# Recurrence gates of a hybrid encoder block: two blocks side by side in the array's rows, their halves brought together by transfers within SBUF, and one square less

## The chip, the core and the metric

The kernel runs on one core of one Trainium2 chip. The metric is device time in microseconds. Three runs of the kernel before took 1136.99, 1137.01 and 1138.92 us, a median of 1137.01 us. One further execution was profiled: it took 1136.66 us, of which 1134.9 us are the span from the first to the last instruction of the program.

The engines are called TensorE (PE in the rows; PEld is its weight load), VectorE (DVE), ScalarE (ACT), GpSimd (POOL) and SyncE (SP). SyncE only issues transfers here; GpSimd clears a few columns and issues some transfers.

## The reference

One layer on 512 tokens of 1024 features, all in float32: a feed-forward half step, a mixer and a second feed-forward half step. The mixer projects the normed input to seven parts. Two of them are attended over a token grid; one goes through a depthwise convolution and then through two gated linear recurrences, one forward in time and one backward:

```python
def _rglru_scan(xc, w_gates, b_gates, lam):
    xb = xc.reshape(B_, S, LRU_BLOCKS, LRU_BLOCK)           # 16 blocks of 64 features
    gates = jnp.einsum('bsni,gnio->gbsno', xb, w_gates)     # each block has its own 64 x 64 weights
    gates = gates + b_gates[:, None, None, :]
    r = jax.nn.sigmoid(gates[0])
    i = jax.nn.sigmoid(gates[1])
    log_a = -LRU_C * r * jax.nn.softplus(-lam)
    a = jnp.exp(log_a)
    bx = jnp.sqrt(-jnp.expm1(2.0 * log_a)) * (i * xc)
    _, h = lax.associative_scan(_lin_combine, (a, bx), axis=1)   # h_t = a_t h_(t-1) + bx_t
```

The gates r and i are 64 x 64 products: features of one block only see features of the same block. The two directions have weights of their own, so that 2 directions x 2 gates x 16 blocks of 64 x 64 weights meet 512 tokens.

## The kernel before

Features lie on the 128 partitions, so that the 1024 features are 8 feature tiles (f = 0 to 7) of 128 x 512, each of two blocks. Matrices of float32 are split into a rounded part and a rest (wh and wl for weights, xh and xl or ch and cl for data), and every product is three matmuls: wh by xh, wh by xl, wl by xh (mm3, L144). Weights stream in pieces of 128 x 1024 through load_w (L132): a transfer by SyncE into wraw, ScalarE's copy to wh (L118), VectorE's difference to wl (L121). There are four buffers each of wh and wl, and three of wraw.

The stages are: first feed-forward, the projection to the recurrence's input (wxr, L645, one piece of 24 matmuls for each f), the projections of q, k and v in two halves (wqkv, L667 to L669, 24 matmuls for a piece), three gate projections, the output projection and the second feed-forward. The recurrence and the attention are generators ("lanes") that weave() advances by a few steps behind each piece of a projection, so many steps per piece as RATE tells (4 for "lru" behind a piece of wxr, 3 behind a piece of the first q, k and v). A scheduler sets the final order of each engine's instructions; every engine works its own list from top to bottom and waits at an instruction whose inputs or buffers are not there.

The recurrence is made in two parts of four feature tiles each (LRU_F = 4). In each, lru() (L584) first makes the gates of one f and direction after the other. For f and direction d it does for g = 0 (r) and g = 1 (i): three matmuls of the full array, whose weights are 128 x 128 with two 64 x 64 blocks on the diagonal and zeros beside them, into one of four aux banks of PSUM; one sigmoid by ScalarE out of that bank (L607). Then VectorE multiplies i by the convolved input (L612) and ScalarE makes th = tanh(8 sp r) (L614), with sp the softplus. After the eight pairs of gates come, for each, a = exp(-8 sp r) (L618), its square (L621), (a*a + 1) * th, which is 1 - a*a (L622); then the roots (L625), the product of root and gated input (L627) and the scans (L633, L635).

In the text a gate group is one f with one direction. The eight groups of the first part (tiles 0 to 3) stand between pieces of wxr for f = 5 to 7, those of the second part (tiles 4 to 7) between pieces 8 to 12 of q, k and v. ch and cl of a tile (L591) must be there before its groups, the bank must have been emptied by the sigmoid that used it last.

Of the kernel before, what the change touches and what calls it, by code (L numbers as in the profile page):

```python
# [9 lines left out]
F32 = mybir.dt.float32  # L10
F32R = mybir.dt.float32r
AF = mybir.ActivationFunctionType
# [4 lines left out]
P = 128  # L17
T = 512
# [34 lines left out]
GB_BATCH = (range(0, 4), range(4, 6), range(6, 7), range(7, 8))  # L53

LRU_F = 4

ATT_LAG = 1, 2

# [9 lines left out]
def block_kernel(ctx: ExitStack, tc, a, out):  # L68
# [18 lines left out]
    def big_t(dt=F32, shape=(P, T), n="b"):  # L87
        return big.tile(list(shape), dt, tag="big", bufs=NBIG, name=nm(n))
# [7 lines left out]
    def aux_t():  # L96
        return aux.tile([P, T], F32, tag="aux", name=nm("aux"))
# [34 lines left out]
    def load_w(src, n, act=True):  # L132
        raw = raw_t()
        H, L = hl_t()
        s = slice(0, n)
        ld = nc.sync.dma_start(raw[:, s], src[:, s])
        if nld[0] < 8:
            tc.keep_in_program_order(ld)
        nld[0] += 1
        with tc.high_priority():  # L140
            split(raw[:, s], H[:, s], L[:, s], act)
        return H, L
# [53 lines left out]
        nc.scalar.activation(r, ps, AF.Copy)  # L196
        return r, rcol, vx

    def after(i, prev):

        i, prev = getattr(i, "ins", i), getattr(prev, "ins", prev)
        tc.add_manual_dep(i, prev.name, mybir.DependencyInfo(
            mybir.DependencyClass.NoSync, mybir.DependencyReason.DATA), reason="order")


    mark = {}
# [341 lines left out]
    sp8 = const.tile([P, 16], F32, name="sp8")  # L548
    nc.vector.tensor_scalar(sp8, sp, 8.0, None, ALU.mult)
# [30 lines left out]


    last_act = [None]

    def lru(fs):  # L584
        un = []
        cuts = {}

        def cut(f):
            if f in fs:
                cuts[f] = big_t(F32R, n="ch"), big_t(F32R, n="cl")  # L590
                split(xc[f], *cuts[f])  # L591

        cut(fs[0])
        for f in fs:
            gH, gL = load_w(a["wgate"][f], T)
            cut(f + 1)
            cH, cL = cuts.pop(f)
            yield
            for d in range(2):
                rt = []  # L600
                for g in range(2):
                    q = d * 2 + g
                    s = slice(q * P, (q + 1) * P)
                    ps = aux_t()
                    mm3(ps, gH[:, s], gL[:, s], cH, cL, True, True)
                    t = big_t(n="gate")
                    i = nc.scalar.activation(t, ps, AF.Sigmoid, bias=small[:, C_BG + f * 4 + q : C_BG + f * 4 + q + 1])  # L607
# [4 lines left out]
                nc.vector.tensor_tensor(ix, ix, xc[f], ALU.mult)  # L612
                th = big_t(n="th")
                tanh = nc.scalar.activation(th, r, AF.Tanh, scale=sp8[:, f * 2 + d : f * 2 + d + 1])  # L614
# [287 lines left out]
def layouts(inp):  # L902
# [28 lines left out]
    bd = np.zeros((KT, P, 4, P), wg.dtype)  # L931
    for b in range(16):
        s = slice((b % 2) * 64, (b % 2) * 64 + 64)
        bd[b // 2, s, :, s] = wg[:, :, b].reshape(4, 64, 64).transpose(1, 0, 2)
    o["wgate"] = bd.reshape(KT, P, 4 * P)
    col = lambda v: np.asarray(v).reshape(-1, KT, P).transpose(2, 1, 0).reshape(P, -1)
    o["small"] = con(np.concatenate([
        col(f("norm_ffn1")[0]), col(f("norm_mix")[0]), col(f("norm_ffn2")[0]),
        col(f("conv_w")[0]), col(f("conv_b")[0]),
        col(f("lru_b_gates")[0].reshape(4, D)), col(f("lru_lambda")[0]),  # L940
        np.tile(f("q_norm")[0], 2)[:, None], np.tile(f("k_norm")[0], 2)[:, None]], 1))


# [31 lines left out]
```

## Time and profile before

| what | value |
|---|---|
| median of three runs | 1137.01 us |
| the profiled execution, span of it | 1136.66 us, 1134.9 us |
| TensorE busy in the span | 1126.8 us (99%) |
| VectorE, ScalarE, GpSimd busy | 837.1, 617.3, 19.3 us |
| matmuls on the program's lines | 6874 |
| first part of the gates (from the first gate matmul to the first of q, k and v) | 384.21 to 409.58 us |
| second part (first to last gate matmul) | 453.1 to 480.3 us |

The profile's page sums up each engine's busy time, follows the chain of work that ended last back from the end, and lists the costliest groups of instructions with the mean of one. Other views show the same execution by stretches of time, by tile, or in order of time with the start of each instruction. A matmul's duration there includes the time in which it passes through the array, while the next has started; what one costs in a stream is the distance between two starts. A released wait stands in brackets behind the row.

### The profile page before, as it was taken

The numbers are of one execution on the slowest core, as the hardware profiler recorded it, in microseconds if no ns is written. First come the engines' busy times: TensorE is split into PE (matmuls) and PEld (weight loads), VectorE is DVE, ScalarE is ACT, GpSimd is POOL, SyncE is SP. The second block draws the span as 40 slices with busy tenths as digits, with TensorE's granted clock in tenths as the row PEclk, the third lists the DMA queues.
The fourth block names the chain that finished last, engine by engine and source line by source line (L and its number), as shares of the span: only waits on it lengthen the run. The fifth ranks groups of instructions, "written<-read, shape, count | busy, mean of one in ns | idle before, by whom it ended". The sixth has DMA issues, their size and how long they took to land.

```text
span 1134.9 us, 17275 instructions
## 1 busy us (share of the span) xinstructions
PE 1126.8 (99%) x6874; PEld 994.4 (88%) x6874; DVE 837.1 (74%) x1288; ACT 617.3 (54%) x924; POOL 19.3 (2%) x52
## 2 busy tenths in 40 slices
PE   9999999999999999999999999999999999999998
PEld 7899999988888888888788887778999999998886
DVE  7898888884836779788855577758688888894542
ACT  8554544563624696995564266756445545464330
POOL 0000000000000000010110000000000000000000
PEclk9999999999999999999999999999999999999999
DMA  8242333443333352353443232345123333253421
GB/s 274 81 131 80 122 97 109 132 133 103 121 102 104 98 169 68 124 165 93 137 143 103 93 102 90 107 167 186 56 80 124 95 108 116 89 171 94 130 75 38
DMA packets 43554, 130.70 MB, mean 115 GB/s; under 512 B 5968, under 2 KB 8272, under 8 KB 43472
## 3 DMA queue, kind: packets, MB, share of 16 engines
q1 hardware_dynamic: 39600, 119.36, 33.6%
q0 software_dynamic: 3296, 9.97, 2.9%
q8 instruction: 54, 0.88, 0.3%
q10 hardware_dynamic: 576, 0.26, 0.1%
q14 instruction: 28, 0.23, 0.1%
HBM read 121.17 MB, written 8.39 MB: 114 GB/s over the span
## 4 chain that ended last, share of the span: by engine, by line
PE 95%; DVE 3%; ACT 2%; issue 0%; DMA 0%; DVEq 0%; ACTq 0%
PE acc L260 29%; PE acc L146 11%; PE acc L145 11%; PE acc L147 10%; PE aux L260 5%; PE aux L145 4%; PE aux L146 4%; PE aux L147 4%; PE acc L668 3%; PE acc L667 3%; PE acc L669 3%; PE aux L796 1%; DVE wl L121 1%; PE aux L785 1%; DVE so L769 1%; ACT wh L118 1%
## 5 line engine op out<-in xcount | busy, mean ns | idle before, releaser
L118 ACT ACTIVATE wh<-wraw 128x1024 fp32r<-128x1024 f32 (+3 forms) x242 | 241.4, 1000 | 323.5 <-PE acc L260 98.5
L121 DVE TENSOR_TENSOR wl<-wraw,wh 128x1024 fp32r<-128x1024 f32 (+3 forms) x254 | 291.5, 1151 | 131.0 <-ACT wh L118 130.4
L260 PE MATMUL acc<-s,wh 128*128 128x256 f32 x1216 | 220.6, 283 | 0.0
L260 PEld LDWEIGHTS acc<-s,wh 128*128 128x128 f32 x1216 | 188.8, 190 | 0.0
L260 PE MATMUL acc<-s,wl 128*128 128x256 f32 x608 | 172.1, 283 | 0.0
L145 PE MATMUL acc<-xh,wh 128*128 128x512 f32 x304 | 120.4, 396 | 0.0
L146 PE MATMUL acc<-xl,wh 128*128 128x512 f32 x304 | 119.5, 393 | 0.0
L147 PE MATMUL acc<-xh,wl 128*128 128x512 f32 x304 | 118.9, 391 | 0.0
L260 PEld LDWEIGHTS acc<-s,wl 128*128 128x128 f32 x608 | 115.8, 190 | 0.0
L260 PE MATMUL acc<-xh,wl 128*128 128x256 f32 x304 | 86.1, 283 | 0.0
L260 PE MATMUL acc<-xl,wh 128*128 128x256 f32 x304 | 86.1, 283 | 0.0
L260 PE MATMUL acc<-xh,wh 128*128 128x256 f32 x304 | 86.0, 283 | 0.0
L667 PE MATMUL acc<-wh,xh 128*128 128x512 f32 x192 | 75.5, 393 | 0.0
L668 PE MATMUL acc<-wh,xl 128*128 128x512 f32 x192 | 74.8, 390 | 0.0
L669 PE MATMUL acc<-wl,xh 128*128 128x512 f32 x192 | 74.8, 389 | 0.0
L294 DVE TENSOR_TENSOR wraw<-wraw,pair 128x1024 f32<-128x1024 f32 x57 | 69.6, 1221 | 0.8
L145 PE MATMUL aux<-hh,wh 128*128 128x512 f32 x176 | 68.5, 389 | 0.0
L146 PE MATMUL aux<-hl,wh 128*128 128x512 f32 x176 | 68.5, 389 | 0.0
L147 PE MATMUL aux<-hh,wl 128*128 128x512 f32 x176 | 68.5, 389 | 0.0
L146 PE MATMUL acc<-hl,wh 128*128 128x512 f32 x176 | 68.5, 389 | 0.0
L145 PE MATMUL acc<-hh,wh 128*128 128x512 f32 x176 | 68.5, 389 | 0.0
L147 PE MATMUL acc<-hh,wl 128*128 128x512 f32 x176 | 68.5, 389 | 0.0
(195 smaller groups left out, 2221.5 us busy)
## 6 DMA issues: line engine op xcount, KB each, us to landing
wraw<-wqkv SPq DMA_DIRECT2D x24, 512.0 KB, 3.6
wraw<-wg SPq DMA_DIRECT2D x24, 512.0 KB, 3.5
wraw<-w1d SPq DMA_DIRECT2D x22, 512.0 KB, 3.6
wraw<-w2d SPq DMA_DIRECT2D x22, 512.0 KB, 3.6
pair<-w2s SPq DMA_DIRECT2D x20, 512.0 KB, 3.6
wraw<-w2s SPq DMA_DIRECT2D x20, 512.0 KB, 3.6
wraw<-w1s SPq DMA_DIRECT2D x18, 512.0 KB, 3.6
pair<-w1s SPq DMA_DIRECT2D x18, 512.0 KB, 3.6
```

The source lines that it names most:

```text
L118: nc.scalar.activation(H, raw, AF.Copy)
L121: nc.vector.tensor_tensor(L, raw, H.bitcast(F32), ALU.subtract)
L145: nc.tensor.matmul(ps, wh, xh, start=first, stop=False)
L146: nc.tensor.matmul(ps, wh, xl, start=False, stop=False)
L147: nc.tensor.matmul(ps, wl, xh, start=False, stop=last)
L260: nc.tensor.matmul(o, w_[:, c], x_, start=first and m + k == 0 and w_ is H and x_ is xh_, stop=m + k == 4 and w_ is L, skip_group_check=True)
L294: nc.vector.tensor_tensor(t, t, o, ALU.add)
L667: nc.tensor.matmul(pss[j], xh[kk][:, tj], H[:, s], start=kk == 0, stop=False)
L668: nc.tensor.matmul(pss[j], xl[kk][:, tj], H[:, s], start=False, stop=False)
L669: nc.tensor.matmul(pss[j], xh[kk][:, tj], L[:, s], start=False, stop=kk == KT - 1)
L769: nc.vector.tensor_tensor_reduce(so[:, cs], ps[hp][:, cs], bm[:, BTYPE[n]], -1.0, 3.0e38, ALU.add, ALU.min, nmx[:, i : i + 1])
L785: nc.tensor.transpose(pT[:, q * P : (q + 1) * P], pt[:, q * P : (q + 1) * P], ident)
```

## The change

Four things change in lru() and in the layout of two inputs.

1. The gate weights hold no zeros any more: wgate[f] is 128 x 256 in place of 128 x 512, with block 2f in rows 0 to 63 and block 2f + 1 in rows 64 to 127, and the 64 columns of r beside the 64 of i for each direction. A gate group is now three pairs of matmuls. The two of a pair have 64 rows each, use rows 0 to 63 and rows 64 to 127 of the array, and write two PSUM banks, one for each block: the bank of block b holds r of that block in its upper 64 partitions and i in its lower 64. The two of a pair and the three pairs are held in that order; the first also waits until the banks of the group before the last are both empty.
2. The two sigmoids of a group go to the two halves of one tile `both` (128 x 2 x 512, from the four buffers of the tag "pair"), which holds r above i for one block and for the other. Four transfers of 64 x 512 each, issued by GpSimd, bring them to r and i of the whole feature tile.
3. The product of i and the input and the tanh of a group are written out two groups later (LRU_LAG = 2).
4. tanh has half the argument, th = tanh(4 sp r) = (1 - a) / (1 + a), so that 1 - a*a = th * (1 + a)^2. VectorE multiplies the gated input by (a + 1) where it multiplied th before, the root is taken of th itself, and the square of a is gone. The biases are laid out to match.

```diff
@@ lru
-            gH, gL = load_w(a["wgate"][f], T)
+            gH, gL = load_w(a["wgate"][f], 2 * P)
...
             for d in range(2):
-                rt = []
-                for g in range(2):
-                    q = d * 2 + g
-                    s = slice(q * P, (q + 1) * P)
-                    ps = aux_t()
-                    mm3(ps, gH[:, s], gL[:, s], cH, cL, True, True)
-                    t = big_t(n="gate")
-                    i = nc.scalar.activation(t, ps, AF.Sigmoid, bias=small[:, C_BG + f * 4 + q : C_BG + f * 4 + q + 1])
+                c = slice(d * P, (d + 1) * P)
+                ps = [aux_t() for _ in range(2)]
+                mm = None
+                for W, X in ((gH, cH), (gH, cL), (gL, cH)):
+                    for b in (0, 1):
+                        o = slice(b * HD, (b + 1) * HD)
+                        prev, mm = mm, nc.tensor.matmul(
+                            ps[b], W[o, c], X[o], start=W is gH and X is cH, stop=W is gL)
+                        if prev is not None:
+                            after(mm, prev)
+                        elif len(evicted) > 1:
+                            after(mm, evicted[-2], True)
+                q = C_BG + f * 4 + d * 2
+                both = pair_t()
+                for b in range(2):
+                    i = nc.scalar.activation(both[:, b], ps[b], AF.Sigmoid, bias=small[:, q + b : q + b + 1])
                     if last_act[0] is not None:
                         after(i, last_act[0])
-                    rt.append(t)
-                r, ix = rt
-                nc.vector.tensor_tensor(ix, ix, xc[f], ALU.mult)
-                th = big_t(n="th")
-                tanh = nc.scalar.activation(th, r, AF.Tanh, scale=sp8[:, f * 2 + d : f * 2 + d + 1])
-                un.append((f, d, r, ix, th))
+                evicted.append(i)
+                r, ix = (big_t(n="gate") for _ in range(2))
+                for g, t in enumerate((r, ix)):
+                    for b in range(2):
+                        nc.gpsimd.dma_start(t[b * HD : (b + 1) * HD], both[g * HD : (g + 1) * HD, b])
+                got.append((f, d, r, ix))
+                if len(got) > LRU_LAG:
+                    tanh = use(*got.pop(0))
                 yield
+        for t in got:
+            tanh = use(*t)
+        yield
         for f, d, r, ix, th in un:
             exp = nc.scalar.activation(r, r, AF.Exp, scale=sn8[:, f * 2 + d : f * 2 + d + 1])
             after(exp, tanh)
-            sq = big_t(n="a2")
-            nc.scalar.activation(sq, r, AF.Square)
-            nc.vector.scalar_tensor_tensor(th, sq, 1.0, th, ALU.add, ALU.mult)
+            nc.vector.scalar_tensor_tensor(ix, r, 1.0, ix, ALU.add, ALU.mult)
```

In use() stand the product of ix with xc[f] and the tanh with sp4 = 4 sp in place of sp8.

Three places of the new order bear on the prediction. The numbers in the names tell the tiles of one program apart.

TensorE, the first gate groups, tile 0 with both directions (ch_624 and cl_625 are its two parts, aux the banks). Before:

```order
L145 MATMUL aux_631_3914<-ch_624_3900,wh_627_3905 128x512
L145 MATMUL aux_633_3920<-ch_624_3900,wh_627_3905 128x512
L145 MATMUL aux_636_3929<-ch_624_3900,wh_627_3905 128x512
L145 MATMUL aux_638_3935<-ch_624_3900,wh_627_3905 128x512
L146 MATMUL aux_631_3914<-cl_625_3901,wh_627_3905 128x512
L147 MATMUL aux_631_3914<-ch_624_3900,wl_628_3906 128x512
L146 MATMUL aux_633_3920<-cl_625_3901,wh_627_3905 128x512
```

Now:

```order
L618 MATMUL aux_631_3914<-ch_624_3900,wh_627_3905 128x512
L618 MATMUL aux_632_3915<-ch_624_3900,wh_627_3905 128x512
L618 MATMUL aux_636_3931<-ch_624_3900,wh_627_3905 128x512
L618 MATMUL aux_637_3932<-ch_624_3900,wh_627_3905 128x512
L618 MATMUL aux_631_3914<-cl_625_3901,wh_627_3905 128x512
L618 MATMUL aux_632_3915<-cl_625_3901,wh_627_3905 128x512
L618 MATMUL aux_631_3914<-ch_624_3900,wl_628_3906 128x512
L618 MATMUL aux_632_3915<-ch_624_3900,wl_628_3906 128x512
```

The number of gate matmuls is the same, 96. Those that follow each other now form pairs. They stand in 11 runs between matmuls of the projections (12, 12, 2, 4, 6, 2, 10 in the first part, four times 12 in the second); before there were 9 runs (12, 12, 6, 12, 6 and four times 12).

ScalarE, around the high part of tile 2 (ch_644), which the fifth gate group needs. Before:

```order
L607 ACTIVATE gate_639_3939<-aux_638_3935,small_78 128x512
L614 ACTIVATE th_640_3942<-gate_637_3933,sp8_3675 128x512
L118 ACTIVATE ch_644_3950<-xc_611_3815 128x512
L118 ACTIVATE wh_698_4142<-wraw_697_4141 128x1024
L576 ACTIVATE xc_651_3989<-xp_650_3985,small_78 128x512
```

Now:

```order
L627 ACTIVATE pair_654_4006<-aux_652_3998,small_78 128x512
L627 ACTIVATE pair_654_4006<-aux_653_3999,small_78 128x512
L120 ACTIVATE wh_704_4176<-wraw_703_4175 128x1024
L120 ACTIVATE ch_644_3954<-xc_611_3815 128x512
L627 ACTIVATE pair_660_4026<-aux_658_4018,small_78 128x512
```

ch_644 now stands behind the sigmoids of the third group (pair_654) and behind the weights of the last piece of wxr (wh_704).

VectorE, around the low part of the same tile (cl_645). Before:

```order
L121 TENSOR_TENSOR wl_685_4106<-wraw_683_4104,wh_684_4105 128x512
L612 TENSOR_TENSOR gate_639_3939<-gate_639_3939,xc_599_3735 128x512
L121 TENSOR_TENSOR cl_645_3951<-xc_611_3815,ch_644_3950 128x512
L121 TENSOR_TENSOR wl_699_4143<-wraw_697_4141,wh_698_4142 128x1024
```

Now:

```order
L123 TENSOR_TENSOR wl_689_4130<-wraw_687_4128,wh_688_4129 128x256
L593 TENSOR_TENSOR gate_635_3926<-gate_635_3926,xc_599_3735 128x512
L123 TENSOR_TENSOR wl_705_4177<-wraw_703_4175,wh_704_4176 128x1024
L123 TENSOR_TENSOR cl_645_3955<-xc_611_3815,ch_644_3954 128x512
```

gate_635 is i of the first gate group, which now comes by transfers; cl_645 stands behind its product and behind the rest of the weights.

More of the change, by code (lines that the diff above doesn't have):

```diff
@@ L55 @@
 LRU_F = 4
+LRU_LAG = 2
 ATT_LAG = 1, 2
@@ L197, in rstd, with after @@
         return r, rcol, vx
-    def after(i, prev):
+    def after(i, prev, sync=False):
         i, prev = getattr(i, "ins", i), getattr(prev, "ins", prev)
         tc.add_manual_dep(i, prev.name, mybir.DependencyInfo(
-            mybir.DependencyClass.NoSync, mybir.DependencyReason.DATA), reason="order")
+            mybir.DependencyClass.Sync if sync else mybir.DependencyClass.NoSync, mybir.DependencyReason.DATA), reason="order")
     mark = {}
@@ L582, in block_kernel, with use @@
     last_act = [None]
+    evicted = []
     def lru(fs):
         un = []
+        got = []
         cuts = {}
+        def use(f, d, r, ix):
+            nc.vector.tensor_tensor(ix, ix, xc[f], ALU.mult)
+            th = big_t(n="th")
+            un.append((f, d, r, ix, th))
+            return nc.scalar.activation(th, r, AF.Tanh, scale=sp4[:, f * 2 + d : f * 2 + d + 1])
         def cut(f):
@@ L930, in layouts @@
     wg = f("lru_w_gates")[0]
[L931 to L935, printed above, removed]
+    o["wgate"] = con(wg.reshape(2, 2, KT, 2, 64, 64).transpose(2, 3, 4, 0, 1, 5)).reshape(KT, P, 4 * 64)
     col = lambda v: np.asarray(v).reshape(-1, KT, P).transpose(2, 1, 0).reshape(P, -1)
+    bg = f("lru_b_gates")[0].reshape(2, 2, KT, 2, 64).transpose(1, 4, 2, 0, 3).reshape(P, 4 * KT)
     o["small"] = con(np.concatenate([
```

6 lines of the change are left out of this document (3 added, 3 removed).

## Prediction

> **What bounds the kernel now.** I read the page first, then stretches of time around the recurrence, then TensorE's own order of time there.
>
> ```profile
> span 1134.9 us, 17275 instructions
> PE 95%; DVE 3%; ACT 2%; issue 0%; DMA 0%; DVEq 0%; ACTq 0%
> ...
> 384.00:410.00 26.00, 26.00 (x114) 21.04 (x113) 21.67 (x30) 24.78 (x38) 2.54 (x8) 1.00 0.61 194
> 410.00:453.00 43.00, 43.00 (x191) 35.60 (x190) 38.20 (x54) 32.11 (x51) 0.00 (x0) 1.00 0.26 79
> 453.00:486.00 33.00, 33.00 (x149) 27.29 (x148) 23.88 (x35) 30.54 (x45) 1.65 (x3) 1.00 0.41 128
> ```
>
> The second row is the chain of waits: 95% of the span runs through TensorE. The last three are stretches (length, then busy time of TensorE, weight load, VectorE, ScalarE, GpSimd; clock, DMA share, GB/s): first part of the gates, what lies between, second part. TensorE has no gap in any of them and the full clock. Array time taken out is therefore span taken out, as long as the others keep up. In the first part that is a question: ScalarE is busy 24.78 of 26 us.
>
> ```profile
> L146 PE MATMUL aux<-cl,wh 128*128 128x512 f32 x32 | 12.5, 390 | 0.0
> L147 PE MATMUL aux<-ch,wl 128*128 128x512 f32 x32 | 12.5, 389 | 0.0
> L145 PE MATMUL aux<-ch,wh 128*128 128x512 f32 x32 | 12.2, 397 | 0.0
> ...
> 384.21 1.22 PE L145 MATMUL aux<-ch,wh 128*128 128x512 f32 x4
> 385.26 0.41 PE L146 MATMUL aux<-cl,wh 128*128 128x512 f32 x1
> 386.87 0.39 PE L147 MATMUL aux<-ch,wl 128*128 128x512 f32 x1
> 390.27 0.39 PE L145 MATMUL aux<-ch,wh 128*128 128x512 f32 x1
> 392.76 0.39 PE L147 MATMUL aux<-ch,wl 128*128 128x512 f32 x1
> 395.03 0.39 PE L145 MATMUL acc<-xh,wh 128*128 128x512 f32 x1
> 395.35 0.50 PE L145 MATMUL aux<-ch,wh 128*128 128x512 f32 x1
> 395.69 0.39 PE L146 MATMUL aux<-cl,wh 128*128 128x512 f32 x1
> ...
> 409.58 0.39 PE L667 MATMUL acc<-wh,xh 128*128 128x512 f32 x1
> ```
>
> There are 96 gate matmuls. From 390.27 to 392.76 eleven starts pass, 0.227 us each: that is the price of one, not the 0.39 for which it is under way. So all gates cost 96 x 0.227 = 21.8 us.
>
> **Array time.** Before, no gate matmul uses half the array, but the attention's scores do:
>
> ```profile
> 524.55 0.39 PE L669 MATMUL acc<-wl,xh 128*128 128x512 f32 x1
> 524.87 0.38 PE L759 MATMUL aux<-kh,qh 64*128 64x256 f32 x2
> 525.09 0.28 PE L759 MATMUL aux<-kl,qh 64*128 64x256 f32 x2
> 525.21 0.28 PE L759 MATMUL aux<-kh,ql 64*128 64x256 f32 x2
> 525.33 0.28 PE L759 MATMUL aux<-kh,qh 64*128 64x256 f32 x2
> ...
> 525.56 0.28 PE L759 MATMUL aux<-kh,ql 64*128 64x256 f32 x2
> 525.78 0.66 PE L733 MATMUL aux<-ident,qk 128*128 128x128 f32 x4
> 526.63 0.48 PE L667 MATMUL acc<-wh,xh 128*128 128x512 f32 x1
> 526.94 0.39 PE L668 MATMUL acc<-wh,xl 128*128 128x512 f32 x1
> ```
>
> Each row of L759 is two matmuls (x2) of 64 rows on the two halves, and 0.12 us later the next two start: 256 columns pass in the time of one matmul, 0.227 x 256/512 = 0.11. So a pair costs as much as one, and I take 0.227 us for a pair of 512 columns: 48 x 0.227 = 10.9 us, a saving of **10.9 us**. Bounds: 0.227 (full overlap) and 0.454 (none).
>
> The switch costs something. From the last full matmul to the first pair 0.32 us pass, 0.09 more than its 0.23. The first pair lasts 0.22 in place of 0.12 (its weights load in the open), 0.10 more. From the last pair to the full array it is 0.22, 0.10 more. The first full matmul behind another kind takes 0.31 (526.63 to 526.94), 0.08 more. Together 0.37 us for a run of pairs between full matmuls; the new order has 11 runs, so **4.1 us** are given back. The Trainium skill says the same thing in TensorEngine Tiling (Array Packing), Key Properties ("Mode switching requires drain"), with no price; its table of theoretical speedup alone ("up to 2x" for 64) would make the sum 10.9 without this term, and the rows decide for 6.8.
>
> **Waits in the first part.** Here the gates feed each other through ScalarE, GpSimd and VectorE, and I follow the new order by hand.
>
> ```profile
> 384.70 1.28 ACT L607 ACT_TABLE_LOAD   x1
> 385.99 0.69 ACT L607 ACTIVATE gate<-aux,small 128x512 f32<-128x512 f32 x1
> 388.08 0.67 ACT L607 ACTIVATE gate<-aux,small 128x512 f32<-128x512 f32 x1
> 388.65 0.71 ACT L614 ACTIVATE th<-gate,sp 128x512 f32<-128x512 f32 x1
> 392.96 1.06 ACT L118 ACTIVATE wh<-wraw 128x1024 fp32r<-128x1024 f32 x1 [0.38 <-PE aux L146]
> ...
> 384.34 0.69 DVE L121 TENSOR_TENSOR cl<-xc,ch 128x512 fp32r<-128x512 f32 x1
> 391.67 0.69 DVE L612 TENSOR_TENSOR gate<-gate,xc 128x512 f32<-128x512 f32 x1
> 394.05 1.23 DVE L121 TENSOR_TENSOR wl<-wraw,wh 128x1024 fp32r<-128x1024 f32 x1 [0.75 <-ACT wh L118]
> ...
> 398.82 2.29 POOL L708 DMA_DIRECT2D bm<-rpb  x4 [0.46 <-issue]
> 564.01 0.77 POOL L695 DMA_DIRECT2D vd<-v  x1 [0.87 <-DVE v L691]
> bm<-rpb POOLq DMA_DIRECT2D x16, 384.0 KB, 4.9
> vs<-vd POOLq DMA_DIRECT2D x6, 256.0 KB, 4.8
> DMA to landing us min/median/max: 3.4/4.9/5.9
> DMA to landing us min/median/max: 3.9/4.8/7.2
> ```
>
> A sigmoid occupies ScalarE 0.57 us (388.08 to 388.65), a weight piece about 1.0, VectorE's operations 0.6 (128 x 512) and 1.15 (128 x 1024). GpSimd issues a transfer in 2.29 / 4 = 0.57 us. Its landing isn't in the trace for 128 KB within SBUF; the nearest rows are 384 KB from HBM (bm, 3.4 to 5.9, median 4.9) and 256 KB (vs, 4.8); the last row is that of vd, 3.9 to 7.2. I take L = 4.2 us from issue, below these medians because it is a third to a half of the bytes, with 3.4 and 5.9 as ends. The Trainium skill's fit in DMA: Bandwidth & Descriptors, Anatomy of one DMA, would be 2.0 us + 131 KB / 436 GB/s = 2.3 us, and the sum by it is the one of L = 3.4 below; no row here is as short.
>
> 1. First run: cl of tile 0 is there at 384.34 + 0.69 = 385.03, but four matmuls ahead of it are now two pairs and end at 384.8: 0.25 us. The run ends at 386.05, the 14 matmuls behind it at 389.3, the second run (0.09 + 0.10 + 6 x 0.227) at 390.9, the 6 matmuls behind it at 392.35.
> 2. The fifth group needs ch of tile 2. ScalarE empties the third group's banks first (390.4 to 391.55), then makes wh of the last wxr piece (to 392.5), then ch (to 393.15): **0.8 us**.
> 3. It needs cl of tile 2 at 394.65 (a pair, the switch back, 4 matmuls). VectorE must first multiply the first group's i. Its last transfer is issued at 388.8 (sigmoid done at 388.2, two issues) and lands at 388.8 + L = 393.0; the product ends at 393.6, the wl behind it at 394.75, cl at 395.4: **0.75 us**, and 1 us more for each us of L above 3.45. Behind that waiting product stand wl, cl and the convolution of tile 5; TensorE waits for cl alone.
> 4. ch of tile 3 is some 0.1 us late in the same way.
>
> Together 1.9 us; the rows above show 0.4 us of such waits before (384.21 to 386.87 is 0.17 longer than 11 x 0.227; 395.03 to 395.69 is 0.20 longer than two), which go. Net **1.5 us** given back. As a check: the 24 pairs of this part with 7 switches alone would cut TensorE's 26 us to 23.2, under ScalarE's 24.78; with the waits it is 24.5.
>
> **The second part** has two groups in every 24 matmuls (12 once), and the uses come 5 to 7 us later. First use: the fourth transfer of its first group is issued some 3.7 us behind the run's start; cl of tile 6, queued behind its product, is wanted 11.9 us behind it: free up to L = 6.9. Last one: the product for the sixth group stands ahead of v's eviction, which TensorE wants for the first piece of the next half; free up to L = 5.0. At 4.2 nothing is lost.
>
> **Other edits.** The 16 squares and two ACT table loads less (the new list has 33 for 35) fall behind the gates, where ScalarE has 32.11 of 43 us of work: nothing, now and with the cover gone. The gate weights' splits are half as wide: 0.3 us each on ScalarE and VectorE, in the chain above. VectorE's operations are as many as before. GpSimd's 64 issues are 64 x 0.57 = 36 us in some 95 us of the recurrence; the padding of the last tile's input is queued behind 16 of them, to about 398, and is wanted after 408; v's transfers come behind the last of them, ahead of the second half as before. The sync wait on the banks is met by then each time (in step 1 by 0.1 us).
>
> **Sum:** -10.9 + 4.1 + 1.5 = **-5.3 us**: the profiled execution's 1136.66 becomes 1131.4. The median of the runs is 0.35 us higher, so I predict 1131.6. With L = 3.4 the gain is 6.0, with 5.0 it is 4.5, with 5.9 2.7 (both slopes count then).
>
> **Rivals.**
> - *Late transfers eat the gain.* Eight issues stand in a row, and rows of four issues land at up to 5.9. With L = 6.2, steps 3 and the sixth group cost 2.0 + 1.2 more: gain 2.1, 1134.9. For it: the waiting product stands in VectorE's list ahead of what TensorE needs. Against: only two of 16 uses are that tight. One way to it is a rule of the Trainium skill, SBUF: State Buffer, two separate sides (the "DVE blocks DMA" trap): a GpSimd transfer's descriptors wait while VectorE runs a two-port operation, 620 ns becoming some 3100. The trace has one such meeting, an issue at 564.01 of 0.77 us beside a cast of L120 that starts at 563.95; that is 0.2 over 0.57. No L120 cast runs in the recurrence, so by the rows it is worth nothing here.
> - *Slower by the same wait.* Step 3 and the sixth group together cancel the gain from L = 7.3 on; at L = 9 the kernel takes about 1140. Against: no GpSimd landing of these sizes but one (7.2, of vd) is over 5.9.
> - *The pairs don't overlap* (the change doesn't do what it says): the 10.9 us are gone, 1142.5. Against: all rows of L759.
> - *TensorE is no longer the bound:* ScalarE's 24.78 us in the first part would leave 24.2 after the splits, a gain of 1.8 there, which is no less than the 1.5 I count.
>
> **How the numbers follow.** A difference under 0.2% (2.3 us) can't be told from none. The forecast with L from 3 to 5.2 (gain 4.2 to 6.5): 0.66. Late transfers (5.2 to 7.3, gain 0 to 4.2): 0.18, of which 0.11 above 2.3 us. Slower by the wait 0.06, no overlap 0.04. Something not listed: 0.06, a third of it each way. So faster 0.66 + 0.11 + 0.02 = 0.79, same 0.07 + 0.03 = 0.10, slower 0.11. The range goes from a gain of 7.5 (switches cheaper, no waits) to one of 1.5: 1129.2 to 1135.6.
>
> **What would show it.** Gate rows of 64*128 128x512 shapes with two starts each 0.23 us, a run of 12 taking 1.75 us with its switches; q, k and v starting about 408.0 in place of 409.58 and the second half of them 5.3 us earlier than before; transfers of gate landing in about 4 us; VectorE's gate product waiting for a transfer, and TensorE 0.5 to 1 us for cl and ch of tile 2. Wrong if pairs start one behind the other, if landings are past 6 us, or if ScalarE's sigmoids hold up the banks.

## The result, and the profile after

The changed kernel takes 1149.12 us (median of four executions, 1148.96 to 1150.33), the kernel before 1137.0: a ratio of 1.0107, 95% interval 1.0095 to 1.0119. It is 12.1 us slower. Forecast were 1131.6 us, with a range of 1129.2 to 1135.6. The profiled execution has a span of 1147.2 us, 12.3 more than before.

Two stretches of the kernel after, the first part of the gates and the start of the second half of q, k and v (length, then busy time of TensorE, weight load, VectorE, ScalarE, GpSimd; granted clock, DMA share, GB/s):

```profile
384.00:410.00 26.00, 22.61 (x98) 14.70 (x98) 15.49 (x21) 17.86 (x27) 11.74 (x27) 0.87 0.71 199
...
486.00:500.00 14.00, 9.13 (x28) 6.99 (x28) 8.62 (x11) 5.01 (x7) 6.06 (x11) 0.76 0.92 238
```

TensorE has gaps now in both (22.61 of 26 us busy, 9.13 of 14), and the granted clock falls to a mean of 0.87 and 0.76, where every stretch before had 1.00. The view of waits for the gates and q, k and v, of TensorE, then of VectorE and of GpSimd (us in total, times, longest):

```profile
PE acc L691 <- DVE v L715: 4.9, 1, 4.9
PE aux L618 <- DVE cl L123: 2.7, 1, 2.7
PE acc L691 <- ACT qk L704: 1.1, 2, 0.8
...
DVE gate L593 <- DMA gate<-pair: 21.9, 11, 4.5
...
POOL gate L634 <- DMA gate<-pair: 9.3, 7, 2.0
```

TensorE waits for VectorE, and VectorE stands 21.9 us at the product of i and the input (L593) until a transfer has landed. TensorE in order of time:

```profile
389.53 0.39 PE L149 MATMUL acc<-xh,wl 128*128 128x512 f32 x1
389.85 0.50 PE L618 MATMUL aux<-ch,wh 64*128 64x512 f32 x2
390.19 0.40 PE L618 MATMUL aux<-cl,wh 64*128 64x512 f32 x2
390.42 0.40 PE L618 MATMUL aux<-ch,wl 64*128 64x512 f32 x2
...
391.11 0.40 PE L618 MATMUL aux<-ch,wl 64*128 64x512 f32 x2
391.44 0.50 PE L147 MATMUL acc<-xh,wh 128*128 128x512 f32 x1
391.78 0.40 PE L148 MATMUL acc<-xl,wh 128*128 128x512 f32 x1
...
394.87 0.40 PE L147 MATMUL acc<-xh,wh 128*128 128x512 f32 x1
397.93 0.79 PE L618 MATMUL aux<-cl,wh 64*128 64x512 f32 x2 [2.66 <-DVE cl L123]
...
399.67 0.63 PE L149 MATMUL acc<-xh,wl 128*128 128x512 f32 x1
400.10 0.63 PE L147 MATMUL acc<-xh,wh 128*128 128x512 f32 x1
...
403.94 0.40 PE L147 MATMUL acc<-xh,wh 128*128 128x512 f32 x1
...
413.59 0.39 PE L691 MATMUL acc<-wh,xh 128*128 128x512 f32 x1
...
488.31 0.39 PE L693 MATMUL acc<-wl,xh 128*128 128x512 f32 x1
493.57 0.80 PE L691 MATMUL acc<-wh,xh 128*128 128x512 f32 x1 [4.87 <-DVE v L715]
```

The pairs do what was forecast: 0.23 us from one to the next, and 0.40 us for a run's switches (0.09 + 0.11 + 0.10 + 0.11 over 0.227 at the four places). But the stall at 394.87 costs 2.83 us over a matmul's own 0.23, and behind it the starts are 0.43 us apart (399.67 to 400.10) up to 403.94, where a matmul's duration is back from 0.63 to 0.40. The stall at 488.31 costs 5.03, and twelve starts 0.427 apart follow up to 499.29. q, k and v start at 413.59, 4.0 us later than before; forecast was 1.6 earlier. What VectorE does at the two stalls:

```profile
395.45 0.69 DVE L593 TENSOR_TENSOR gate<-gate,xc 128x512 f32<-128x512 f32 x1 [4.47 <-DMA gate<-pair]
396.06 1.22 DVE L123 TENSOR_TENSOR wl<-wraw,wh 128x1024 fp32r<-128x1024 f32 x1
397.19 0.69 DVE L123 TENSOR_TENSOR cl<-xc,ch 128x512 fp32r<-128x512 f32 x1
...
491.03 0.69 DVE L593 TENSOR_TENSOR gate<-gate,xc 128x512 f32<-128x512 f32 x1 [2.31 <-DMA gate<-pair]
491.64 1.22 DVE L123 TENSOR_TENSOR wl<-wraw,wh 128x1024 fp32r<-128x1024 f32 x1
492.77 1.40 DVE L715 TENSOR_SCALAR v<-acc,rcol 128x512 f32<-128x512 f32 x2
```

Both times it is the pattern of the forecast's step 3: product, wl, then what TensorE waits for (cl of tile 2; v). The landings, from the view of transfers of 384 to 500 us (KB each, median us from issue to landing), and of the tile gate over all, then over its four issues from 401.5 to 404 us alone, while hardly any weight moves:

```profile
wraw<-wqkv SPq DMA_DIRECT2D x19, 512.0 KB, 6.2
gate<-pair POOLq DMA_DIRECT2D x64, 128.0 KB, 5.8
...
DMA to landing us min/median/max: 2.2/5.8/8.2
...
DMA to landing us min/median/max: 2.2/2.6/2.7
```

Two rows of the same view before, the weights and v's own transfers, of twice the bytes:

```profile
wraw<-wqkv SPq DMA_DIRECT2D x20, 512.0 KB, 3.6
...
vd<-v POOLq DMA_DIRECT2D x4, 256.0 KB, 5.4
```

Four transfers in a row land in 2.2 to 2.7 us in a quiet stretch; over all the median is 5.8, and the weights lose as well.

A balance of TensorE between 380 and 620 us, from the distances between starts, each less what its shape takes (0.227 us for 512 columns; a pair counts as one): pairs -10.9; switches 11 x 0.40 = +4.4; the two long stalls +7.9; half clock behind them +5.7 (2.9 and 2.8); shorter waits (ch of tile 2, q's evictions, the first k of the attention) +3.5. That is +10.6. By the starts of the same matmuls before and after, TensorE is 0.25 us behind at 381 and 11.9 at 567, so 11.6 arise in between, and 1 us of them has no place in this balance. The other 0.4 of the 12.3 lies behind TensorE's last matmul.

### The profile page after: what moved, and what is told of

It reads as the page before. It is cut to its first block, busy times and chain, and to the rows that moved or that the text cites. A ratio compares the mean times of both kernels' runs of the same rounds, so it can differ in the third digit from the quotient of the medians.

```text
span 1147.2 us, 17448 instructions
## 1 busy us (share of the span) xinstructions
PE 1128.0 (98%) x6874; PEld 987.7 (86%) x6874; DVE 834.2 (73%) x1288; ACT 604.0 (53%) x906; POOL 52.3 (5%) x116
## 4 chain that ended last, share of the span: by engine, by line
PE 55%; ACT 3%; DVE 3%; DMA 2%; issue 1%; POOL 0%; POOLq 0%; ACTq 0%; DVEq 0%
PE acc L262 15%; PE acc L148 7%; PE acc L147 7%; PE acc L149 7%; PE acc L691 3%; PE aux L262 3%; PE acc L692 2%; PE acc L693 2%; DMA gate<-pair 2%; PE aux L148 2%; PE aux L147 2%; PE aux L149 2%; PE aux L820 1%; DVE wl L123 1%; ACT wh L120 1%
## 5 line engine op out<-in xcount | busy, mean ns | idle before, releaser
L120 ACT ACTIVATE wh<-wraw 128x1024 fp32r<-128x1024 f32 (+3 forms) x242 | 238.9, 992 | 336.5 <-PE acc L262 98.5
L123 DVE TENSOR_TENSOR wl<-wraw,wh 128x1024 fp32r<-128x1024 f32 (+3 forms) x254 | 289.1, 1142 | 126.4 <-ACT wh L120 125.6
L148 PEld LDWEIGHTS acc<-xl,wh 128*128 128x128 f32 x304 | 57.7, 190 | 13.0 <-issue 1.7
L147 PEld LDWEIGHTS acc<-xh,wh 128*128 128x128 f32 x304 | 57.7, 190 | 12.8 <-PE aux L618 0.7
```

What stands on the lines that cost most here:

```text
L120: nc.scalar.activation(H, raw, AF.Copy)
L123: nc.vector.tensor_tensor(L, raw, H.bitcast(F32), ALU.subtract)
L147: nc.tensor.matmul(ps, wh, xh, start=first, stop=False)
L148: nc.tensor.matmul(ps, wh, xl, start=False, stop=False)
```

## The experiments

Theory 1: the product waits for late transfers in VectorE's list, ahead of what TensorE needs, and a stall costs more than its length. Theory 2: the pairs cost more than thought. Theory 3: the traffic itself costs, since it makes the weights late. Times are medians; each stands beside the kernel before on the same chip (1136.7 to 1137.1 us).

### No transfers (no_move)

This kernel leaves the transfers out: each sigmoid writes a whole tile, half of which then holds values of the other gate.

```diff
-                both = pair_t()
-                for b in range(2):
-                    i = nc.scalar.activation(both[:, b], ps[b], AF.Sigmoid, bias=small[:, q + b : q + b + 1])
+                r, ix = (big_t(n="gate") for _ in range(2))
+                for b, t in enumerate((r, ix)):
+                    i = nc.scalar.activation(t, ps[b], AF.Sigmoid, bias=small[:, q + b : q + b + 1])
...
-                r, ix = (big_t(n="gate") for _ in range(2))
-                for g, t in enumerate((r, ix)):
-                    for b in range(2):
-                        nc.gpsimd.dma_start(t[b * HD : (b + 1) * HD], both[g * HD : (g + 1) * HD, b])
```

> The changed kernel without its 64 transfers: the two sigmoids of a group write two tiles, and these are used as r and i as they are. So half of each tile holds the wrong gate (the output is not the layer's), the work of every engine but GpSimd is the same. Theory 1 (the transfers land too late, VectorE's product waits for them, and TensorE stalls behind it and then runs at half clock): both stalls (2.8 us at 394.9, 5.0 us at 488.3) and the slow stretches behind them are gone; 96 matmuls at half price save 10.9 us, 9 runs of pairs at 0.37 us give back 3.3, so 1137.0 - 7.6 = about 1129.5 us, 1128.5 to 1131.5. Theory 2 (the pairs and their switches cost more than the rows of the scores showed): still 1137 or more.

Measured: 1132.59 us against 1137.09, ratio 0.9962 (0.9948 to 0.9977). Both stalls and the slow stretches are gone, the clock is 1.00. So theory 2 falls, and the transfers, with all that they make others wait for, cost 16.5 us. The gain is 4.5, not 7.6. In the gates TensorE still waits 1.0 us for a bank that a sigmoid has not emptied; where the other 2.1 went isn't shown:

```profile
PE aux L618 <- ACT gate L627: 1.0, 2, 0.8
```

### The same traffic, read by nobody (unread, unread_small)

The run without transfers, with 64 transfers added that bring nothing that an operation reads:

```diff
+                dump = [big_t(n="dump") for _ in range(2)]
+                for g, t in enumerate(dump):
+                    for b in range(2):
+                        after(nc.gpsimd.dma_start(t[b * HD : (b + 1) * HD], xc[f][g * HD : (g + 1) * HD]), i, True)
```

> As the run without transfers, but with 64 transfers of 64x512 issued by GpSimd behind the sigmoids, from xc into tiles that nobody reads: the same traffic, and nobody waits for it. Theory 1 (the wait for the landing is what costs): within 1.5 us of the run without transfers, about 1130 us. Theory 3 (the traffic itself costs, because it makes the weights late; wqkv pieces land 5.6 us behind their issue in the changed kernel against 3.7 before, one after 10.9): 3 to 10 us slower than the run without transfers, with TensorE waiting for wh or wl.

In the second run each of these moves `:16` columns in place of 512:

> As the run with transfers that nobody reads, with 16 columns in each in place of 512 (4 KB for 128 KB); the number of transfers, their issues and their waits for each other stay. Theory 3a (the bytes cost: the weights land late): weights land in about 3.7 us again and the time is that of the run without transfers, 1132 to 1134 us. Theory 3b (the issues, or the order of the work that came with them, cost): within 2 us of the run with whole transfers, 1142 to 1145 us.

Measured: 1143.70 us (ratio 1.0058, 1.0041 to 1.0075) with whole transfers, 1133.40 (0.9973, 0.9964 to 0.9982) with small ones. TensorE's waits of 384 to 530 us and the weights' row with whole transfers:

```profile
PE acc L691 <- DVE v L715: 3.2, 1, 3.2
PE aux L618 <- DVE cl L123: 3.2, 1, 3.2
...
wraw<-wqkv SPq DMA_DIRECT2D x19, 512.0 KB, 6.4
```

and the weights' row with small ones, where neither wait is left:

```profile
wraw<-wqkv SPq DMA_DIRECT2D x21, 512.0 KB, 3.8
```

64 issues and their waits cost about 1 us (3.4 gained in place of 4.5). Whole transfers, 8 MB beside the weights, cost 10.3 more, and my forecast of theory 1 for this run (1130) missed. TensorE loses some 9.1 of these at the same two kinds of place as in the change: 3.2 us for a cl of the second part (to 458.34), 3.2 for v (to 492.74), and some 2.7 by starts 0.43 us apart behind the first. That looks like theory 3, but the trace doesn't show late weights at either place: ScalarE's copies of the weights (wh) wait for TensorE to free their buffers, and none of them waits for a weight's landing. VectorE has come late to cl and v, with a list in another order (between the two runs TensorE's list differs in 14 places); it never waits for one of the added transfers, but later tiles take over the buffers that these fill. So traffic beside a product that isn't read can cost 10 us here, and whether by bytes, by buffers or by order is not parted.

### Product two groups later still (lag4)

```diff
-LRU_LAG = 2
+LRU_LAG = 4
```

> The changed kernel with LRU_LAG = 4 in place of 2: product and tanh of a group are written out four groups later. Theory 1: transfers still land in 5 to 8 us, but no cl stands behind a waiting product in the first part; the stall of 2.8 us and its slow stretch (about 2.9 us) go, 5 to 6 us gained there. At the end of each part four products come in a row, so the wait ahead of v's eviction (5.0 us plus 3 us of slow clock) can stay: 1143 us if it stays, 1132 to 1135 if it goes too. Theory 3 (traffic): no change, 1148 to 1150.

Measured: 1147.26 us (1.0088, 1.0073 to 1.0103). VectorE at the first stall:

```profile
395.97 0.69 DVE L593 TENSOR_TENSOR gate<-gate,xc 128x512 f32<-128x512 f32 x1 [5.25 <-DMA gate<-pair]
...
397.72 0.69 DVE L123 TENSOR_TENSOR cl<-xc,ch 128x512 fp32r<-128x512 f32 x1
```

The product still stands ahead of cl. Where it is written out in the program did not set its place; by what rule the scheduler placed it, the run doesn't show. So the run did not test what it was made for.

### Issued by ScalarE (act_queue)

```diff
-                        nc.gpsimd.dma_start(t[b * HD : (b + 1) * HD], both[g * HD : (g + 1) * HD, b])
+                        nc.scalar.dma_start(t[b * HD : (b + 1) * HD], both[g * HD : (g + 1) * HD, b])
```

> The changed kernel with the 64 transfers issued by ScalarE behind its own sigmoids, and not by GpSimd. Theory 1a (the queue of GpSimd is what is slow: its issues of 0.52 us and at most eight in flight): transfers land in 2 to 3.5 us and the stalls go: 1131 to 1135 us. Theory 1b (the 16 DMA engines are what is slow, with 512 KB of a weight piece ahead in each): they land in 4 to 8 us as before, and the time stays at 1144 to 1152 us, more if ScalarE pays for the issues.

Measured: 1170.32 us (1.0290, 1.0274 to 1.0305). Landings, and four issues in ScalarE's queue:

```profile
gate<-pair ACTq DMA_DIRECT2D x48, 128.0 KB, 5.2
...
427.42 2.44 ACTq L634 DMA_DIRECT2D gate<-pair  x4
```

Another queue lands hardly sooner (5.2 us in place of 5.8), so it is not GpSimd's way of issuing that is slow. An issue takes 0.6 us on ScalarE too (2.44 / 4), in whose list sigmoids and evictions stand: TensorE waits 11.3 us there for two evictions of q and k.

### Products held behind cl and v (pin2, pin4)

All 64 transfers stay. The products are ordered behind the last cl and v that the program has written out by then, an order within VectorE's list without a wait. pin4 has LRU_LAG = 4 as well.

```diff
         def use(f, d, r, ix):
-            nc.vector.tensor_tensor(ix, ix, xc[f], ALU.mult)
+            p = nc.vector.tensor_tensor(ix, ix, xc[f], ALU.mult)
+            for m in ("cl", "v"):
+                if m in mark:
+                    after(p, mark[m])
...
-                split(xc[f], *cuts[f])
+                mark["cl"] = split(xc[f], *cuts[f])
...
-                nc.vector.tensor_scalar(t, ps, rcol[:, j : j + 1], None, ALU.mult)
+                mark["v"] = nc.vector.tensor_scalar(t, ps, rcol[:, j : j + 1], None, ALU.mult)
```

> The changed kernel with LRU_LAG = 4, and each product held, in VectorE's list alone, behind the last cl that was cut so far and, once v is written, behind v. All 64 transfers stay, with their traffic. Theory 1 (VectorE's list: a product that waits for its transfer stands ahead of cl and of v): the two long stalls and their slow stretches (2.8 + 2.9 and 5.0 + 3.0 us) are gone, 1132 to 1136 us. Theory 3 (the traffic itself costs, as the run with transfers that nobody reads suggested): 1142 or more, with waits for weights in their place.

> The changed kernel with LRU_LAG = 2 as it is, and only each product held, in VectorE's list, behind the last cl cut so far and behind v once v is written. If the place in that list is the cause (theory 1): both long stalls go as in the run with LRU_LAG = 4, 1135 to 1139 us. If the two groups more of distance were what helped there: a stall of 2 us or more stays, 1141 to 1148 us.

Measured: pin4 1136.80 us (1.0003, 0.9993 to 1.0012), pin2 1145.14 (1.0074, 1.0058 to 1.0091). In pin4 VectorE still stands at the product, and the weights land later than in the change (7.2 us in place of 6.2):

```profile
DVE gate L593 <- DMA gate<-pair: 12.0, 6, 3.0
...
wraw<-wqkv SPq DMA_DIRECT2D x21, 512.0 KB, 7.2
```

but no stall of TensorE over 0.8 us is left up to 500 us (two of 1.2 and 1.3 us come behind), and the clock is 1.00. So the whole 12.1 us of loss go when the products stand behind cl and v, with as many transfers as in the change. Against lag4, from which pin4 differs by this order alone, it is 10.2 us. The scheduler made other lists anew from it, though: in pin4 ScalarE's too, where the tanh of the gates stand later. In pin2 ScalarE's list is that of the change, VectorE's differs in 8 places, and so its first stall is the clean case. Theory 3 in its strong form (1142 or more) falls. pin2 takes away the first stall alone: its last products were written out before v was there, and nothing held them behind it:

```profile
488.58 0.69 DVE L593 TENSOR_TENSOR gate<-gate,xc 128x512 f32<-128x512 f32 x1 [2.49 <-DMA gate<-pair]
...
490.32 2.06 DVE L718 TENSOR_SCALAR v<-acc,rcol 128x512 f32<-128x512 f32 x3
```

There the stall of 5.05 us stays, and TensorE waits 1.73 for another cl. By these runs the first stall with what follows is worth some 4 us (1149.1 to 1145.1; 5.7 with its slow starts, less the new wait), the one at v some 8 (to 1136.8). At v the changed kernel's own trace shows the order at work: the transfer that was issued at 483.76 lands at 490.93, the product starts at 491.03, wl, whose wh had been there since 486.9, at 491.64, v at 492.77, and TensorE goes on at 493.57.

### Straight to its place by ScalarE (pairshift)

```diff
-                both = pair_t()
+                r, ix = (big_t(n="gate") for _ in range(2))
...
-                    i = nc.scalar.activation(both[:, b], ps[b], AF.Sigmoid, bias=small[:, q + b : q + b + 1])
+                    for g, t in enumerate((r, ix)):
+                        o, s = slice(b * HD, (b + 1) * HD), slice(g * HD, (g + 1) * HD)
+                        i = nc.scalar.activation(t[o], ps[b][s], AF.Sigmoid, bias=small[s, q + b : q + b + 1])
...
-                        nc.gpsimd.dma_start(t[b * HD : (b + 1) * HD], both[g * HD : (g + 1) * HD, b])
```

> The changed kernel with no transfer and the right result all the same: four sigmoids of 64 partitions in place of two of 128 write each half straight to its place, two of them across to the other half of the partitions. 32 ScalarE operations of 0.57 us more, 18 us, 9 of which the squares had freed. If ScalarE's slack takes them: near the run without transfers (1132.6), 1133 to 1136 us. If ScalarE becomes the bound beside the gates (24.8 of 26 us busy there before, 9 us more now): 5 to 8 us lost in the first part, 1138 to 1142 us.

Measured: 1152.91 us (1.0144, 1.0129 to 1.0159), worse than both cases expected. ScalarE is the bound of the first part, 25.48 of 26 us:

```profile
384.00:410.00 26.00, 23.45 (x112) 15.71 (x111) 17.24 (x24) 25.48 (x37) 2.55 (x8) 1.00 0.57 182
```

Sigmoids that follow each other start 0.70 us apart, 0.57 in the changed kernel, where they have 128 partitions; the expectation counted 0.57. TensorE waits 7.1 us for its sigmoids, 3.7 for v and 1.6 for cl, and there are three stretches of slow starts. So v and cl can come late without any transfer, too.

### What a stall costs (stall)

The kernel before, with TensorE's first matmul of five pieces of the output projection held until a chain of memsets is through:

```diff
+STALL = [0, 1, 2, 3, 0, 4, 0, 6]
...
+        t = big_t(n="blank")
+        for k in range(n):
+            b = nc.gpsimd.memset(t, 0.0)
+            if k == 0:
+                after(b, prev_mm[-1], True)
+        after(mm, b, True)
```

> The kernel before, with TensorE held up at the start of five pieces of the output projection by a chain of 1, 2, 3, 4 and 6 memsets of 128x512 on GpSimd (about 0.55 us each and some 0.6 us for the two hand-overs), so stalls of about 1.2, 1.7, 2.3, 2.8 and 3.9 us. Theory 1 counts a stall at its length alone: 12 us in all. The two stalls of the changed kernel (2.8 and 5.0 us) say that more is lost: some 15 matmuls behind each start 0.427 us apart in place of 0.227, 3 us more for each. By that the two or three longest here cost about 3 us more than their length, and those under 2 us nothing more.

Measured: 1151.88 us (one execution), 15.1 over the kernel before. Over a matmul's own time the five stalls cost 0.87, 1.44, 1.97, 2.55 and 3.72 us, 10.6 together. In order of time, the third and the fourth, and the fifth's first row:

```profile
763.47 0.50 PE L147 MATMUL acc<-yh,wh 128*128 128x512 f32 x1 [1.80 <-POOL blank L156]
...
764.15 0.63 PE L149 MATMUL acc<-yh,wl 128*128 128x512 f32 x1
764.57 0.63 PE L147 MATMUL acc<-yh,wh 128*128 128x512 f32 x1
...
778.64 0.50 PE L147 MATMUL acc<-yh,wh 128*128 128x512 f32 x1 [2.39 <-POOL blank L156]
778.98 0.39 PE L148 MATMUL acc<-yl,wh 128*128 128x512 f32 x1
...
793.38 0.50 PE L147 MATMUL acc<-yh,wh 128*128 128x512 f32 x1 [3.56 <-POOL blank L156]
```

Behind the third and the fifth, seven starts each are 0.427 us apart; the fourth, longer than the third, has none. A slow stretch costs 1.6 us here, 2.8 and 2.9 in the changed kernel. The five stalls and two slow stretches make 13.8 of the 15.1 us. The expectation missed in that the third, under 2 us, costs 1.6 more, and the fourth, over 2, nothing more. So a stall can cost about twice its length, but its length alone does not tell whether it will.

### Half the bytes (two_moves, swap, second_swap), the second part alone (second_part)

Half of what the sigmoids write lies in its place already. two_moves and swap are pin4 with 32 transfers. two_moves brings the two displaced halves to a spare tile and works on halves:

```diff
-                        nc.gpsimd.dma_start(t[b * HD : (b + 1) * HD], both[g * HD : (g + 1) * HD, b])
...
+                nc.gpsimd.dma_start(turn[:HD], r[HD:])
+                nc.gpsimd.dma_start(turn[HD:], ix[:HD])
```

swap has the first of these, and two groups later it moves the second half into the place that became free:

```diff
+            nc.gpsimd.dma_start(r[HD:], ix[:HD])
```

> The run with LRU_LAG = 4 and pinned products, with half the bytes: the first bank's r and the second bank's i already lie in their partitions, so only the other two halves are moved (32 transfers in place of 64), and product, tanh and exp work on the two halves of 64 partitions apart: 16 VectorE operations of 0.6 us and 32 ScalarE operations of 0.57 us more. Theory 3 (what is left of the loss comes from the bytes): gate transfers land in about 4 us in place of 6.6, weights in 4 to 5 in place of 7.2, and 1 to 3 us of the 4.2 us between that run and the one without transfers come back: 1134 to 1136 us. Rival: the 18 us more of ScalarE work hold up q's and k's evictions: 1138 to 1142 us.

> The run with LRU_LAG = 4 and pinned products, with 32 transfers in place of 64 and ScalarE's work as in the change: the lower half of the first bank's tile goes to a spare tile, then the upper half of the second bank's goes to the place that became free; only the product is split in two halves (16 VectorE operations of 0.6 us more). If the bytes make up what the pinned run lacks against the run without transfers (4.2 us): landings of 4 to 5 us and 1133.5 to 1136 us. If it is the order of the work, or the waits that the issues bring: 1136 to 1139 us, whatever the landings are.

second_part is pin4 for tiles 4 to 7, with the full array and no transfers for tiles 0 to 3; second_swap is swap in the same way.

```diff
+                if fs[0] >= LRU_F:
...
+                else:
+                    for g in range(2):
+                        s = slice((d * 2 + g) * P, (d * 2 + g + 1) * P)
+                        mm3(ps[g], gH[:, s], gL[:, s], cH, cL, True, True)
```

> Pairs, transfers and pinned products (LRU_LAG = 4) for tiles 4 to 7 alone; tiles 0 to 3 make their gates on the full array as before, with no transfer. The new tanh and the missing square stay for all. By the run without transfers the second part is worth 5.45 - 4 x 0.37 = 4.0 us of array time, less what the transfers there cost: 0.7 to 2 us. Forecast 1134.5 to 1136 us. Rival (the traffic beside q, k and v costs as much as the pairs save): 1136.5 to 1138.

> The same half of the transfers, for tiles 4 to 7 alone; tiles 0 to 3 on the full array as before. Against the run with all four transfers there (1136.2 us): 1134.5 to 1135.7 us if the bytes count, 1136 to 1137 if they don't.

Measured: two_moves 1148.84 us (1.0104, 1.0089 to 1.0119), swap 1151.93 (1.0153, 1.0130 to 1.0175), second_part 1136.17 (0.9993, 0.9984 to 1.0003), second_swap 1144.70 (1.0074, 1.0056 to 1.0092). The landings got shorter as expected, in swap for example

```profile
wraw<-wqkv SPq DMA_DIRECT2D x19, 512.0 KB, 4.5
pair<-gate POOLq DMA_DIRECT2D x16, 128.0 KB, 4.8
gate<-gate POOLq DMA_DIRECT2D x16, 128.0 KB, 2.8
```

and the times got worse. In two_moves ScalarE's added work holds q's evictions (TensorE waits 6.2 us for them), in swap TensorE waits 6.7 us for q's eviction and 5.2 for banks. In second_swap ScalarE's list shows why:

```profile
501.02 0.72 ACT L611 ACTIVATE th<-gate,sp 128x512 f32<-128x512 f32 x1 [5.61 <-DMA gate<-gate]
...
512.33 0.57 ACT L730 ACTIVATE qk<-acc 128x512 f32<-128x512 f32 x1
```

The last transfer is issued behind three of v's on GpSimd; the tanh that needs it holds ScalarE for 5.6 us, eight exp and the first roots follow, and the eviction of q that TensorE waits for (6.0 us) comes at 512.33. It is the first fault in another list: I had held the products, and not the tanh. So these runs do not tell what the bytes are worth: the 4.5 us between pin4 and no_move, each against the kernel before on its chip, stay open (the expectations have 4.2, from plain medians). second_part is no different from the kernel before within what can be told; no version here that computes the layer clearly beats it.

### The square alone (no_square)

```diff
-                tanh = nc.scalar.activation(th, r, AF.Tanh, scale=sp8[:, f * 2 + d : f * 2 + d + 1])
+                tanh = nc.scalar.activation(th, r, AF.Tanh, scale=sp4[:, f * 2 + d : f * 2 + d + 1])
...
-            sq = big_t(n="a2")
-            nc.scalar.activation(sq, r, AF.Square)
-            nc.vector.scalar_tensor_tensor(th, sq, 1.0, th, ALU.add, ALU.mult)
+            nc.vector.scalar_tensor_tensor(ix, r, 1.0, ix, ALU.add, ALU.mult)
```

> The kernel before with one part of the change alone: tanh of half the argument and (a + 1) times the gated input in place of the square. 16 ScalarE operations fewer, behind the gates, where ScalarE had 32 of 43 us of work. Every theory: no change, 1136 to 1138 us.

Measured: 1136.63 against 1136.74 us (1.0000, 0.9990 to 1.0009). No change, as said.

## Why the prediction was wrong

- *Array time, -10.9 us:* right. A pair costs 0.23 us.
- *Switches, +4.1:* right within a tenth, 0.40 for a run in place of 0.37.
- *Waits in the first part, +1.5:* the step that failed first is step 3, and in it the value of L. I took 4.2 us, below the medians of larger transfers with other neighbours; the transfer that counts was issued at 389.58 and landed at 395.35, 5.8 us. By the step's own line that alone makes 2.35. It was also issued 0.8 us later than the step has it, and TensorE wanted cl 0.45 later (395.1), which together makes 2.7; 2.83 were measured. The mechanism was right, the term too small. ch of tile 2 was late by 0.70, 0.8 forecast.
- *The second part, "free up to L = 5.0":* failed. Its transfer was issued at 483.76 and landed at 490.93, 7.2 us, which by that line makes 2.2; measured were 5.03. A row of before lay nearer than those I took: v's transfers in this very stretch (issued at 484 to 487) took 5.0 to 7.2 us, median 5.4. I also had the issues follow their sigmoids at once. But the program's transfers post eight counters in turn, so that a ninth waits for the first, and with landings of 6 to 8 us GpSimd waits too (9.3 us in all): the issue was late as well as the landing. The product ahead of it in VectorE's list had waited 3.4 us itself. How the other 2.8 us divide between the two isn't shown.
- *A term that was missing:* a stall has a price beyond its length. Half clock cost 5.7 us, more than the whole gain forecast, and no row of before showed it, since TensorE never stood still for as much as 1 us there.
- *Contention:* I let the landing vary, and not the weights. They went from 3.6 to 6.2 us. What that costs by itself isn't shown: unread lost 10 us beside late weights, but not by waits for them, and pin4 lost nothing with weights at 7.2.
- *Squares, nothing:* right, by its own run (no_square).
- *Rivals:* "slower by the same wait" was what happened, with the place and mechanism given; its price (1140 at L = 9) lacked the late issues and the clock, and its chance of 0.06 rested on the landings of before. It was reached at a median landing of 5.8 us, where the sum has a gain left. The pairs do overlap, and ScalarE did not become the bound until it was given more work (pairshift).

The sum itself has a small slip: 1136.66 - 5.3 + 0.35 is 1131.7.

By the runs the loss divides so, against the kernel before on the same chip: no_move -4.5 us, the array's part with hardly anything to wait for; pin4 0.0; pin2 +8.4; the change +12.1. Shown is that the products' place ahead of cl and v makes the two stalls: for the first by pin2, for the second by the trace of the change, and by pin4, which takes both away but has other lists changed too. Not shown is how the 4.5 us between no_move and pin4 divide between late weights and other waits.

## What to carry to other kernels

An operation whose input comes by a transfer holds everything behind it in its engine's list, so look first at what stands behind it there, and see where the scheduler put it, not where the program wrote it. Take a landing time from transfers with as much traffic beside them as the new ones will have, and count how many may be under way at once. Price a stall of TensorE at up to twice its length when the gain in view is only a few microseconds (1.97 + 1.6 and 2.83 + 2.9 here).

## What the runs showed of the hardware

TensorE's clock falls behind stalls that are short. In the run with stalls the granted clock is 0.50 for 3.41 us from 763.89, behind an idle time of 1.80, and for 3.41 us from 794.61, behind 3.56; behind 2.39 it stays at 1.00. In the changed kernel it is 0.50 for 6.83 us from 397.11 and for 6.83 from 492.68. These are one and two times 3.41 us, and from 763.89 to 794.61 it is nine times 3.413. So take the run with stalls in windows of 3.413 us, with 763.89 on a border. The idle 1.80 us lie whole in the window before the border, where TensorE is busy 1.60 of 3.41 us. The 2.39 fall on both sides of a border at 777.54, and the two windows are busy 2.12 and 2.31. Of the 3.56, the window that ends at 794.61 has 2.19 and is busy 1.23. In the changed kernel the windows that end at 397.11 and 492.68 are busy 1.57 and 0.00; both stalls last beyond the border, and there the half clock lasts two windows. By these rows a window that is idle for half its length is enough, and where a stall falls in the windows decides its price. Where between 1.3 and 1.8 idle us the bound lies, these rows don't tell.

The Trainium skill, TensorE: Matmul & The Clock Gate, Part 1, tells of a window of 3413 ns that runs freely. The lengths of the stretches and the borders agree with it; its condition of at least one idle window does not agree with the row of 1.80 us.

The landing of a transfer of 128 KB within SBUF depends on its neighbours: 2.2 to 2.7 us in a quiet stretch, 5.8 in the median, 8.2 at most. The Trainium skill's fit in DMA: Bandwidth & Descriptors, Anatomy of one DMA, which gave 2.3 us in the prediction, agrees with the quiet rows alone.
